# Moving the norm-factor sums and transposes of a hybrid attention layer later in TensorE's order, with one product and four operand rebuilds re-timed

## The chip, the cores and the metric

The kernel runs on one core of a Trainium2 chip. The metric is the device time of one execution in microseconds, as the median of several runs. Engines are named as in the profile: PE is TensorE (PEld its weight loads), DVE VectorE, ACT ScalarE, POOL GpSimd, and SP the engine that issues most DMAs. Each engine takes its instructions strictly in the order in which they were built.

## The reference

One encoder layer on x of 1024 tokens by 2048 features: RMSNorm, one input projection, eight retention heads, eight windowed attention heads, gates, an output projection, the residual and a last RMSNorm.

```python
h = rms_norm(x, norm_w)                 # x * rsqrt(mean(x*x) + eps) * w, per token
proj = h @ w_in                         # 2048 x 6656
rq, rk, rv, rg, aq, ak, av, ag = jnp.split(proj, splits, axis=-1)
y_ret = retention_branch(rq, rk, rv, ...) * silu(rg)
y_att = window_attention_branch(aq, ak, av, sink) * silu(ag)
out = rms_norm(x + concat([y_ret, y_att]) @ w_out, final_norm_w)
```

All of it is in float32; the kernel writes each factor of a big product as a rounded high part and a low rest and makes three matmuls of each pair.

## The kernel before, in words

**The projection.** `units` (L205) lists the work: a unit is one block of 512 output columns and one half (`part`) of the 2048 features. Columns and features of a unit are halved again, and a unit is made of seven products instead of eight, from sums of the quarters of the weight (`a11`, `a12`, `a21`, `a22`) and sums of the quarters of x (`comb[1]` to `comb[7]`, the tiles `c...` of the profile). "Operand" in this text means one such sum, split into high and low part: on the weight's side the tiles `wH` and `wL` (two of each, so operand n+2 waits until operand n has been used), on x's side `comb[i]`, which `put` (L1127) builds by a cast on ACT (L89) and a subtraction on DVE (L86). Each product takes 24 matmuls of 128x512 in four groups of six. Products 1, 6, 7 and 4 add up in the two PSUM banks X, products 2, 5 and 3 in the two banks Y; between two products on the same banks the sum so far has to be read out by DVE (`evict_rest`, L312, line L93 in the profile, tile `ct`), and PE may not write the bank until then.

**The start.** RMSNorm's factors are not known when the first matmul could run. So the first block, `akv`, is made by eight plain products (`plain`, L354): those on the first 512 tokens with unscaled x, then products 1 and 2 of the second block (`aq0`) and of the third (`aq1`) also unscaled (`early`, L390, banks `ax` and `pj`), then `plain` on the second 512 tokens with scaled x, then the other five products of the second and the third block (`rest`, L414). In `rest` the order is 5, 6, 3, 7, 4. Unscaled results wait in `ct` tiles until `scale_result` (L1131) multiplies them by the factors.

**The factors.** Half of the features come as columns and are squared on ACT (L498) and added on DVE (L93, tile `xx`); `sum_columns` (L507) has PE add them over the partitions by four matmuls with a vector of ones (L510). The other half comes as rows, eight tiles `xt`, squared with a running sum on ACT (L493). `factors_of` (L513) adds both on DVE (L516) and takes the power -0.5 on POOL (L517); `spread` (L1083) copies the factors over 128 columns (L1085); `turn_rows` (L1087) has PE transpose them (L1089, four small matmuls) and ACT copy the result into the tile `rows` (L1090), by which DVE then scales x (`scale`, L1092, line L1094). All this is done twice, first for the second half of the tokens, then for the first.

**The order.** `advance()` (L990) is called after every group of six matmuls of the projection, and each call is one step of a clock. The table of `at(n, ...)` calls (L1149 to L1214) says after which step each piece of work of the start is written into the program; where a call issues matmuls, that also is its place between PE's groups. Steps 1 to 16 are `plain` on the first half, 17 to 32 `early`, 33 to 48 `plain` on the second half, 49 to 68 `rest` of the second block, 69 to 88 that of the third. PE, SP and POOL keep the written order throughout; ACT and DVE keep it until step 66 (`BY_HAND`, L55), and after that the build orders them. `keep(0)` (L519) stores the finished x operands for later, 1 MB at a time; `second_part` (L539) loads the other half of x; `mixed` (L208) builds the weight operands of the second and the third block and, by `then`, reloads each weight quarter once it is free. `rotate` (L559) applies the rotary turn for the attention heads, in pieces that wait `idle(5)` steps between their loads and their first multiplication.

Of the kernel before, what the change touches and what calls it, by code (L numbers as in the profile page):

```python
# [59 lines left out]
def hybrid_layer_kernel(  # L60
# [34 lines left out]
    def sub(dst, a, b):  # L95
        return nc.vector.tensor_tensor(out=dst, in0=a, in1=b, op=ALU.subtract)
# [7 lines left out]
    def behind(it, ins):  # L104

        if it and clock[0] >= BY_HAND:
            tc.keep_in_program_order(ins)
# [4 lines left out]
    def half(i):  # L112
        return slice(i * HALF, (i + 1) * HALF)
# [9 lines left out]
    def start(job):  # L123
        if next(job, True) is None:
            jobs.append(job)
# [4 lines left out]
    def idle(n):  # L130
        for _ in range(n):
            yield
# [59 lines left out]
    def operand(src, pinned=False):  # L192
        wH, wL = (wp.tile([P, M, 2 * P], F32R, name=n, tag=n, bufs=AHEAD) for n in ("wH", "wL"))
        behind(pinned, nc.scalar.copy(out=wH, in_=src))  # L194
        low(wL, src, wH)
        return wH, wL
# [8 lines left out]
    units = [(part, b) for part, blocks in PHASES for b in blocks]  # L205
    w_next = {}

    def mixed(a, then):  # L208

        a11, a12, a21, a22 = (a[q] for q in QUARTERS)  # L210
        s2 = wp.tile([P, M, 2 * P], F32, name="s2", tag="s2")
        sub(a11, a11, a21)
        yield
        add(a21, a21, a22)
        yield
        op = [wp.tile([P, M, 2 * P], F32R, name=n, tag=n, bufs=AHEAD) for n in ("wH", "wL")]
        nc.scalar.copy(out=op[0], in_=a21)
        yield
        sub(s2, a22, a11)
        yield  # L220
        low(op[1], a21, op[0])
        then(2, 1)
        yield op
        yield operand(s2)
        sub(s2, a12, s2)
        then(1, 2)
        yield
        yield operand(s2)
        op = operand(a11)
        then(1, 1)  # L230
        yield op
        op = operand(a22)
        then(2, 2)
        yield op

    def then_of(u):

        def then(n, k):
            if u + 1 < len(units):
                w_next[n, k] = quarter(*units[u + 1], n, k)  # L240
            else:
                place_free(n, k)

        return then

    def operands():

        for u in range(2, len(units)):
            a, then = dict(w_next), then_of(u)
            if u == 2:  # L250
                yield from (op for op in mixed(a, then) if op)
                continue
            a11, a12, a21, a22 = (a[q] for q in QUARTERS)
            yield operand(a11)
            op = operand(a12)
            s2 = wp.tile([P, M, 2 * P], F32, name="s2", tag="s2")
            behind(True, sub(a11, a11, a21))
            sub(s2, a22, a11)
            yield op
            yield operand(s2, True)  # L260
            add(a21, a21, a22)
            op = operand(a21)
            then(2, 1)
# [12 lines left out]
            then(2, 2)  # L276
            yield op
# [68 lines left out]
    ops, ready = operands(), deque()  # L346
    unscaled, rows_of = [], []
    first_banks = {}
# [65 lines left out]
    def rest(b):  # L414

        if b not in held_of:
            first_scaled(b)
        held = held_of[b]
        Y, X = [pj(), pj()], [pj(), pj()]
        for i in (5, 6, 3, 7, 4):  # L420
            if b != units[1][1] or i == 4:
                prepare()
            bank = X if i in ON_X else Y
            products(i, bank, ready.popleft(), comb[i], i in (5, 6), True, lambda a: evict_rest(b, i, a, bank[a], held))
# [64 lines left out]
    def load_first(q, s, m, k0=0, n=M):  # L489
        q.dma_start(out=src0[:, s, k0:k0 + n, half(m)], in_=x_f[s, m][:, k0:k0 + n])  # L490
# [16 lines left out]
    def sum_columns(m, pt):  # L507

        for t in range(4):
            nc.tensor.matmul(pt[:, t:t + 1], columns[m][:, 0, blk(t)], ones, start=True, stop=True)  # L510
        nc.vector.tensor_copy(out=ssx[:, 0, 4 * m:4 * m + 4], in_=pt[:, 0:4])
# [47 lines left out]
    def rotate(pool, table, sets):  # L559

        for m in range(2):
            cs = [pool.tile([P, HALF], F32, name=f"rt{k}") for k in range(2)]
            for k in range(2):
                nc.sync.dma_start(out=cs[k], in_=table[:, k, half(m)])
            for of in sets:
                ts = [pool.tile([P, HALF], F32, name=f"rx{k}") for k in range(2)]
                for t, runs in zip(ts, of):
                    n = runs[0][2]
                    for i, (c, r, _) in enumerate(runs):
                        nc.sync.dma_start(out=t[i * n:(i + 1) * n], in_=pr[c][r:r + n, half(m)])  # L570
                yield from idle(5)
                n = of[0][0][2]
                u = slice(0, n * len(of[0]))
                for t, f in zip(ts, cs):
                    behind(True, nc.vector.tensor_tensor(out=t[u], in0=t[u], in1=f[u], op=ALU.mult))
                yield
                add(ts[0][u], ts[0][u], ts[1][u])
                yield from idle(2)
                for i, (c, r, _) in enumerate(of[0]):
                    nc.sync.dma_start(out=pr[c][r:r + n, half(m)], in_=ts[0][i * n:(i + 1) * n])  # L580
                yield
# [415 lines left out]
    u0, u1, u2 = units[:3]  # L997
    a11 = wp.tile([P, M, 2 * P], F32, name="a11", tag="a11")
# [63 lines left out]
    def load_quarter(n, k):  # L1062
        w_next[n, k] = quarter(*u1, n, k)
# [2 lines left out]
    load_quarter(1, 1)  # L1066
    load_first(nc.sync, 0, 1)
    load_first(nc.sync, 1, 1)
    for t in (4, 5, 6, 7):
        load_row(t)  # L1070
    load_quarter(1, 2)
    load_row(0)
    load_row(1)
    early_quarter(1)
# [12 lines left out]
    def turn_rows(m, pt):  # L1087
        for t in range(4):
            nc.tensor.transpose(pt[:, blk(t)], factors[m][:, blk(t)], ident)  # L1089
        nc.scalar.copy(out=both[:, half(m)], in_=pt)  # L1090
# [43 lines left out]
            nc.vector.tensor_tensor(out=e, in0=e, in1=rows_of[0], op=ALU.mult)  # L1134
            stores.append((True, to, e))

    mixed_first = mixed(w_next, then_of(1))

    def step(n=1):
        for _ in range(n):  # L1140
# [5 lines left out]
    def at(n, what, *args):  # L1146
        plan.setdefault(n, []).append((what, args))

    at(7, lambda: ready.append(operand(w_next[1, 1])))  # L1149
    for n, m in ((8, 0), (11, 1)):  # L1150
# [4 lines left out]
            if i < 3:  # L1155
                at(n + i, square_columns, m, i + 1)
        at(n + 3, add_columns, m, 4)
    at(13, lambda: sum_columns(0, first_banks[0, 1][0]))
    for n, t in ((13, 4), (14, 5), (15, 6), (15, 7), (18, 0), (19, 1), (21, 2), (22, 3)):
        at(n, square_row, t)  # L1160
    at(16, lambda: sum_columns(1, first_banks[0, 1][1]))
    at(16, factors_of, 4, 8)
    at(16, lambda: ready.append(operand(w_next[1, 2])))
    at(16, spread, 1)
    at(19, lambda: turn_rows(1, first_banks[0, 2][0]))
    at(19, hold_second)
    at(19, second_half, 0, "scale")
    at(20, lambda: ready.append(operand(early_w[1])))
    at(21, load_quarter, 2, 1)
    at(23, hold_third)  # L1170
    for k in range(2 * M):
        at(20 + k, second_half, k, "high")
        if k + 1 < 2 * M:
            at(20 + k, second_half, k + 1, "scale")
        at(20 + k, second_half, k, "low")
    at(23, factors_of, 0, 4)
    at(24, spread, 0)
    at(24, lambda: ready.append(operand(early_w[2])))
    at(25, load_quarter, 2, 2)
    at(26, lambda: turn_rows(0, first_banks[u1[1], 2][0]))  # L1180
    at(28, scale_result)
    at(31, scale_result)
    at(37, scale_result)
    at(48, scale_result)
    for k in range(M):
        at(33 + k // 2, scale, 0, k, 0)
    for n in (29, 30, 40, 40, 42, 47, 51):
        at(n, step)
    for j in range(2):
        at(35 + j, sum_of, 5, j)  # L1190
        at(38 + j, sum_of, 6, j)
        at(40 + j, put, 5, j)
        at(45 + j, put, 6, j)
        at(49 + j, sum_of, 7, j)
        at(51 + 2 * j, put, 7, j)
    for n, i in ((40, 5), (45, 6), (51, 7)):
        plan[n].insert(0, (hold, (i, 0)))
    at(44, first_scaled, u1[1])
    at(52, step)
# [7 lines left out]
    at(60, step)  # L1207
    at(61, put, 4, 1)
    for j in range(2):
        at(62 + j, put, 1, j)  # L1210
        at(66 + j, put, 2, j)
    at(62, lambda: start(keep(0)))
    at(69, lambda: start(second_part()))
    at(112, lambda: start(decays()))  # L1214

    def opening():
# [336 lines left out]
    for u in range(len(OUT)):  # L1553
# [4 lines left out]
        for group in LAST if u == 3 else [(i,) for i in PRODUCTS]:  # L1558
            i = group[0]
# [12 lines left out]
            for at, (p, t, j, q) in enumerate(order):  # L1572
# [7 lines left out]
                k = 2 * j + q  # L1580
# [92 lines left out]
```

## Time and profile before

| | |
|---|---|
| median of 3 runs | 1516.34 us (1514.03 to 1517.34) |
| the profiled execution | 1515.38 us, its span 1513.5 us |
| PE busy | 98% of the span |
| DVE, ACT, POOL busy | 74%, 45%, 10% |
| DMA | 316 MB moved, 209 GB/s on average |

A timeline row gives the start, the length, engine, line, operation and tiles, and in square brackets the idle time just before it with what ended that. The windows view gives busy microseconds of each engine in a stretch, with the number of instructions, then the granted PE clock as a share of full speed, the DMA engines' share and GB/s. The view of waits gives, for an engine and a line, whom it waited for, the sum, the number of times and the longest. The rows themselves stand in the prediction.

### The profile page before, as it was taken

The page shows a single profiled execution, that of the slowest core. Times are in us where ns is not written, and L with a number is a line of the kernel's source. Part 1 is how long each engine was busy: PE and PEld are TensorE (multiplying, and loading weights), DVE is VectorE, ACT ScalarE, POOL GpSimd, SP SyncE. Part 2 cuts the span into 40 slices and gives each one's busy share as a digit, 9 for nine tenths or more (in the row PEclk, how much of TensorE's full clock was granted, in tenths as well). Part 3 has the DMA queues.
Part 4 walks back from the last instruction along what each step waited for, and adds up shares of the span by engine and source line. Part 5 has one row for each costly group of instructions (what it writes and reads, how often), then busy time and mean ns, then how long its engine had stood idle before and what let it go on. Part 6 is the DMA issues. An engine that isn't in the chain of part 4 may idle for free.

```text
span 1513.5 us, 19947 instructions
## 1 busy us (share of the span) xinstructions
PE 1484.5 (98%) x7112; PEld 1247.4 (82%) x7112; DVE 1122.6 (74%) x1933; ACT 675.2 (45%) x1093; POOL 149.0 (10%) x176
## 2 busy tenths in 40 slices
PE   9999999999999999999999999999999999999997
PEld 7777888788888888888888788887888878888886
DVE  6897794557768576757988889887656956776766
ACT  7432363224545453533444444444444554542425
POOL 0000001111010000011211100001211102020001
PEclk9999999999999999999999999999999999999999
DMA  8249667888575526798767665689887799495656
GB/s 333 70 139 375 250 222 200 222 204 253 163 215 195 202 97 224 271 324 202 161 173 173 161 197 165 188 290 333 219 246 181 176 207 205 90 208 170 216 175 255
DMA packets 139779, 316.00 MB, mean 209 GB/s; under 512 B 31392, under 2 KB 52256, under 8 KB 130848
## 3 DMA queue, kind: packets, MB, share of 16 engines
q1 hardware_dynamic: 116064, 264.37, 52.5%
q0 software_dynamic: 19728, 36.71, 16.5%
q10 hardware_dynamic: 3888, 13.65, 2.7%
q8 instruction: 56, 0.92, 0.3%
q14 instruction: 43, 0.35, 0.1%
HBM read 195.92 MB, written 127.14 MB: 213 GB/s over the span
## 4 chain that ended last, share of the span: by engine, by line
PE 86%; DVE 5%; DMA 4%; issue 2%; ACT 1%; SPq 1%; POOL 1%; POOLq 0%; DVEq 0%; ACTq 0%
PE pj L102 22%; PE pj L100 22%; PE pj L101 22%; PE ax L101 5%; PE ax L102 5%; PE ax L100 5%; PE ax L882 2%; PE pj L369 1%; DMA pr<-ct 1%; PE ax L669 1%; DVE wL L86 1%; DMA yt<-mix 1%; PE ax L852 1%; DVE c L86 1%; PE ax L933 1%
## 5 line engine op out<-in xcount | busy, mean ns | idle before, releaser
L100 PE MATMUL pj<-c,wH 128*128 128x512 f32 x1384 | 549.1, 397 | 7.5 <-DVE ct L93 4.9
L102 PE MATMUL pj<-c,wL 128*128 128x512 f32 x1384 | 542.1, 392 | 4.9 <-DVE wL L86 4.8
L101 PE MATMUL pj<-c,wH 128*128 128x512 f32 x1384 | 540.6, 391 | 0.0
L102 PEld LDWEIGHTS pj<-c,wL 128*128 128x128 f32 x1384 | 260.6, 188 | 63.6 <-DVE wL L86 8.4
L100 PEld LDWEIGHTS pj<-c,wH 128*128 128x128 f32 x1384 | 260.9, 189 | 58.1 <-issue 5.1
L101 PEld LDWEIGHTS pj<-c,wH 128*128 128x128 f32 x1384 | 260.8, 188 | 49.4
L86 DVE TENSOR_TENSOR wL<-a,wH 128x1024 fp32r<-128x1024 f32 x151 | 184.1, 1220 | 102.3 <-ACT wH L194 52.4
L194 ACT CAST wH<-a 128x1024 fp32r<-128x1024 f32 x121 | 127.1, 1050 | 168.7 <-PE pj L101 134.2
L336 ACT COPY ct<-pj 128x512 f32<-128x512 f32 x184 | 106.9, 586 | 199.3 <-PE pj L102 194.1
L93 DVE TENSOR_TENSOR ct<-pj,ct 128x512 f32<-128x512 f32 x170 | 113.2, 686 | 49.4 <-PE pj L102 46.4
L309 POOL DMA_DIRECT2D pr<-ct x88 | 78.0, 957 | 527.1 <-DVE ct L93 429.8
L86 DVE TENSOR_TENSOR wL<-s,wH 128x1024 fp32r<-128x1024 f32 x56 | 68.4, 1221 | 57.8 <-ACT wH L194 49.9
L100 PE MATMUL pj<-wH,c 128*128 128x512 f32 x224 | 88.0, 393 | 1.4 <-ACT wH L89 1.4
L101 PE MATMUL pj<-wL,c 128*128 128x512 f32 x224 | 87.8, 392 | 0.8 <-DVE wL L86 0.8
L102 PE MATMUL pj<-wH,c 128*128 128x512 f32 x224 | 87.9, 392 | 0.0
L101 PE MATMUL ax<-wL,c 128*128 128x512 f32 x208 | 81.0, 390 | 0.0
L102 PE MATMUL ax<-wH,c 128*128 128x512 f32 x208 | 80.9, 389 | 0.0
L100 PE MATMUL ax<-wH,c 128*128 128x512 f32 x208 | 80.9, 389 | 0.0
L194 ACT CAST wH<-s 128x1024 fp32r<-128x1024 f32 x50 | 52.5, 1051 | 13.6 <-PE pj L101 8.6
L89 ACT CAST wH<-a 128x1024 fp32r<-128x1024 f32 x28 | 29.5, 1053 | 62.0 <-PE pj L102 35.0
L100 PEld LDWEIGHTS pj<-wH,c 128*128 128x128 f32 x224 | 42.5, 190 | 10.7 <-ACT wH L89 1.8
L659 ACT ACTIVATE s<-s,nm 128x385 f32<-128x385 f32 (+1 forms) x64 | 37.6, 589 | 30.2 <-DVE nm L654 27.3
(229 smaller groups left out, 2136.8 us busy)
## 6 DMA issues: line engine op xcount, KB each, us to landing
a<-in_w_in_dram SPq DMA_DIRECT2D x103, 512.0 KB, 5.7
kept<-c SPq DMA_DIRECT2D x28, 1024.0 KB, 7.0
c<-kept SPq DMA_DIRECT2D x28, 1024.0 KB, 8.3
pr<-ct SPq DMA_DIRECT2D x88, 256.0 KB, 5.1
pr<-ct POOLq DMA_DIRECT2D x88, 256.0 KB, 5.9
a<-in_w_out_dram SPq DMA_DIRECT2D x18, 512.0 KB, 4.4
rx<-pr SPq DMA_DIRECT2D x64, 128.0 KB, 5.2
ysrc<-pr ACTq DMA_DIRECT2D x16, 512.0 KB, 5.7
```

The lines of the kernel that those rows point to most:

```text
L86: return nc.vector.tensor_tensor(out=dst, in0=src, in1=high.bitcast(F32), op=ALU.subtract)
L89: behind(pinned, nc.scalar.copy(out=dst_h, in_=src))
L93: nc.vector.tensor_tensor(out=dst, in0=a, in1=b, op=ALU.add)
L100: nc.tensor.matmul(po, aH, bH, start=first, stop=False, **kw)
L101: nc.tensor.matmul(po, aH, bL, start=False, stop=False, **kw)
L102: nc.tensor.matmul(po, aL, bH, start=False, stop=last, **kw)
L194: behind(pinned, nc.scalar.copy(out=wH, in_=src))
L309: nc.gpsimd.dma_start(out=dst, in_=t, accum_op=ALU.add)
L336: nc.scalar.copy(out=t, in_=bank)
L369: nc.tensor.matmul(banks[a], w[:, q, blk(a)], c[:, q], start=first and j == 0, stop=last and j == 2)
L659: nc.scalar.activation(out=s[:, 0:w + 1], in_=s[:, 0:w + 1], func=AF.Exp, scale=-1.0, bias=nm, accum_out=den)
L882: nc.tensor.matmul(p, k_tok[:, c // 2, :, c % 2], vd[:, c, d], start=True, stop=True)
```

## The change

Seven things are edited, all but two of them in the table of steps:

- `sum_columns` goes from steps 13 and 16 to 15 and 18, the first `factors_of` and `spread` from 16 to 18, the first `turn_rows` from 19 to 21, the second from 26 to 30, the second `factors_of` and `spread` from 23 and 24 to 25 and 26; the multiplications of the second half by the factors go two steps later.
- The operand from weight quarter `a12` of the second block is built at step 13 instead of 16, and SP loads that quarter ahead of four of the rows of x instead of behind them.
- `scale_result` is called at 31, 37, 43 and 47 instead of 28, 31, 37 and 48.
- x operand 1 is rebuilt (`put`) at 39 and 40 instead of 62 and 63, x operand 2 at 69 and 70 instead of 66 and 67; the sums 6 and `put(5)` move by one step.
- In the third block `rest` takes the products in the order 5, 6, 7, 3, 4 instead of 5, 6, 3, 7, 4, and `mixed` builds that block's weight operands in the same order (`seventh_first`), with its reload of `a11` ahead of that of `a12`.
- `second_part` starts at 72 instead of 69.
- `rotate` waits six steps instead of five.

```diff
@@ rest
-        for i in (5, 6, 3, 7, 4):
+        for i in (5, 6, 3, 7, 4) if b == units[1][1] else (5, 6, 7, 3, 4):
@@ rotate
-                yield from idle(5)
+                yield from idle(6)
@@ loads
+    load_quarter(1, 2)
     for t in (4, 5, 6, 7):
         load_row(t)
-    load_quarter(1, 2)
@@ the table of steps
-    at(13, lambda: sum_columns(0, first_banks[0, 1][0]))
+    at(13, lambda: ready.append(operand(w_next[1, 2])))
+    at(15, lambda: sum_columns(0, first_banks[0, 1][0]))
...
-    at(26, lambda: turn_rows(0, first_banks[u1[1], 2][0]))
+    at(30, lambda: turn_rows(0, first_banks[u1[1], 2][0]))
...
+        at(39 + j, put, 1, j)
...
-        at(62 + j, put, 1, j)
-        at(66 + j, put, 2, j)
+        at(69 + j, put, 2, j)
...
-    at(69, lambda: start(second_part()))
+    at(72, lambda: start(second_part()))
```

What it does to the built order is shown at three places. The first is PE at the end of `plain` on the first half of the tokens, where the sums over the partitions stand (L369 is a matmul of `plain`, L510 the sums, `ax` the first product of the second block). Before:

```order
L369 MATMUL pj<-c_215,w 128x512 x6
L510 MATMUL pj<-ones,xx 128x1 x4
L369 MATMUL pj<-c_215,w 128x512 x18
L510 MATMUL pj<-ones,xx 128x1 x4
L100 MATMUL ax<-c_214,wH 128x512
```

After it (line numbers past L207 are higher by 7 there; L376 is the matmul of `plain`, L517 the sums):

```order
L376 MATMUL pj<-c_215,w 128x512 x18
L517 MATMUL pj<-ones,xx 128x1 x4
L376 MATMUL pj<-c_215,w 128x512 x6
L100 MATMUL ax<-c_214,wH 128x512
L101 MATMUL ax<-c_214,wH 128x512
```

The first group of sums has gone behind twelve more matmuls of `plain`; the second, which stood ahead of the first `ax` matmul, stands twelve matmuls into that product. The second place is PE in the third block's two early products, where the second transpose of the factors stands (L1089, after it L1096). It leaves the middle of product 1 (`ax` matmuls on `c_214`):

```order
 L101 MATMUL ax<-c_214,wH 128x512
 L102 MATMUL ax<-c_214,wL 128x512
-L1089 MATMUL pj<-ident,factors 128x128 x4
 L100 MATMUL ax<-c_214,wH 128x512
 L101 MATMUL ax<-c_214,wH 128x512
```

and goes into the middle of product 2 (`pj` matmuls on `c_215`):

```order
 L101 MATMUL pj<-c_215,wH 128x512
 L102 MATMUL pj<-c_215,wL 128x512
+L1096 MATMUL pj<-ident,factors 128x128 x4
 L100 MATMUL pj<-c_215,wH 128x512
 L101 MATMUL pj<-c_215,wH 128x512
```

That is 24 matmuls later. The third place is DVE while PE makes products 3, 7 and 4 of the second block (L93 on `pj` reads out the banks; the first pair is product 3's, the second product 7's; `c_214` is x operand 1, `c_215` operand 2, `c_883` operand 4). Before:

```order
L86 TENSOR_TENSOR wL<-a_262,wH 128x1024
L96 TENSOR_TENSOR tt<-src,tt 128x1024 x2
L86 TENSOR_TENSOR c_215<-src,c_215 128x1024
L86 TENSOR_TENSOR c_883<-tt,c_883 128x1024
L93 TENSOR_TENSOR ct<-pj,ct 128x512 x2
L86 TENSOR_TENSOR wL<-a_549,wH 128x1024
L86 TENSOR_TENSOR c_883<-tt,c_883 128x1024
L86 TENSOR_TENSOR c_214<-src,c_214 128x1024 x2
L93 TENSOR_TENSOR ct<-pj,ct 128x512 x2
```

After it (operand 4 is `c_887` there, L419 is `first_scaled` of the third block):

```order
L86 TENSOR_TENSOR wL<-a_262,wH 128x1024
L96 TENSOR_TENSOR tt<-src,tt 128x1024 x2
L419 TENSOR_TENSOR ct<-ax,rows 128x512
L86 TENSOR_TENSOR c_887<-tt,c_887 128x1024
L93 TENSOR_TENSOR ct<-pj,ct 128x512 x2
L86 TENSOR_TENSOR wL<-a_539,wH 128x1024
L86 TENSOR_TENSOR c_887<-tt,c_887 128x1024
L93 TENSOR_TENSOR ct<-pj,ct 128x512 x2
```

Operand 1 has left the place ahead of product 7's read-out (it now stands behind the sums for product 6, before `c_704`, operand 5), operand 2 has gone behind it, and half of `first_scaled` has come in. Further on, the longer wait in `rotate` puts everything that attention and retention issue on PE two groups (twelve matmuls) later against the projection, from the first transposes of attention to the end of retention; ACT and DVE come out in another order there, and in the same one after retention but for a few places.

More of the change, by code (lines that the diff above doesn't have):

```diff
@@ L206, in hybrid_layer_kernel, with mixed @@
     w_next = {}
-    def mixed(a, then):
+    def mixed(a, then, seventh_first):
         a11, a12, a21, a22 = (a[q] for q in QUARTERS)
@@ L224, in mixed, with seventh @@
         yield operand(s2)
+        def seventh():
+            op = operand(a11)
+            then(1, 1)
+            return op
+        if seventh_first:
+            yield seventh()
         sub(s2, a12, s2)
@@ L228, in mixed @@
         yield operand(s2)
-        op = operand(a11)
-        then(1, 1)
-        yield op
+        if not seventh_first:
+            yield seventh()
         op = operand(a22)
@@ L250, in operands @@
             if u == 2:
-                yield from (op for op in mixed(a, then) if op)
+                yield from (op for op in mixed(a, then, True) if op)
                 continue
@@ L1135, in scale_result @@
             stores.append((True, to, e))
[L1137 removed]
+    mixed_first = mixed(w_next, then_of(1), False)
     def step(n=1):
@@ L1157, in hybrid_layer_kernel @@
         at(n + 3, add_columns, m, 4)
-    at(13, lambda: sum_columns(0, first_banks[0, 1][0]))
+    at(13, lambda: ready.append(operand(w_next[1, 2])))
+    at(15, lambda: sum_columns(0, first_banks[0, 1][0]))
     for n, t in ((13, 4), (14, 5), (15, 6), (15, 7), (18, 0), (19, 1), (21, 2), (22, 3)):
         at(n, square_row, t)
[L1161 to L1167, printed above, removed]
+    at(18, lambda: sum_columns(1, first_banks[0, 1][1]))
+    at(18, factors_of, 4, 8)
+    at(18, spread, 1)
+    at(21, lambda: turn_rows(1, first_banks[0, 2][0]))
+    at(20, hold_second)
     at(20, lambda: ready.append(operand(early_w[1])))
+    at(21, second_half, 0, "scale")
     at(21, load_quarter, 2, 1)
@@ L1171, in hybrid_layer_kernel @@
     for k in range(2 * M):
-        at(20 + k, second_half, k, "high")
+        at(22 + k, second_half, k, "high")
         if k + 1 < 2 * M:
[L1174 to L1177, printed above, removed]
+            at(22 + k, second_half, k + 1, "scale")
+        at(22 + k, second_half, k, "low")
     at(24, lambda: ready.append(operand(early_w[2])))
     at(25, load_quarter, 2, 2)
-    at(26, lambda: turn_rows(0, first_banks[u1[1], 2][0]))
[L1181 to L1184, printed above, removed]
+    at(25, factors_of, 0, 4)
+    at(26, spread, 0)
+    at(30, lambda: turn_rows(0, first_banks[u1[1], 2][0]))
+    for n in (31, 37, 43, 47):
+        at(n, scale_result)
     for k in range(M):
         at(33 + k // 2, scale, 0, k, 0)
-    for n in (29, 30, 40, 40, 42, 47, 51):
+    for n in (29, 30, 39, 40, 43, 47, 51):
         at(n, step)
@@ L1190, in hybrid_layer_kernel @@
         at(35 + j, sum_of, 5, j)
-        at(38 + j, sum_of, 6, j)
-        at(40 + j, put, 5, j)
+        at(37 + j, sum_of, 6, j)
+        at(39 + j, put, 1, j)
+        at(41 + j, put, 5, j)
         at(45 + j, put, 6, j)
@@ L1195, in hybrid_layer_kernel @@
         at(51 + 2 * j, put, 7, j)
-    for n, i in ((40, 5), (45, 6), (51, 7)):
+    for n, i in ((41, 5), (45, 6), (51, 7)):
         plan[n].insert(0, (hold, (i, 0)))
```

## The prediction

> **What bounds the kernel now.** I read the head of the page first, then the view of PE's waits, then the windows, and last the timelines of PE, DVE and ACT around each wait.
>
> ```profile
> span 1513.5 us, 19947 instructions
> PE 1484.5 (98%) x7112; PEld 1247.4 (82%) x7112; DVE 1122.6 (74%) x1933; ACT 675.2 (45%) x1093; POOL 149.0 (10%) x176
> PE pj L100 <- DVE ct L93: 4.9, 3, 3.2
> PE pj L102 <- DVE wL L86: 4.8, 5, 1.5
> PE pj L100 <- ACT wH L194: 2.6, 1, 2.6
> PE pj L1089 <- DVE factors L1085: 2.5, 2, 1.9
> PE pj L510 <- DVE xx L93: 0.8, 1, 0.8
> ```
>
> PE is the bound: 1513.5 - 1484.5 = 29 us of the span is all that it stands still. The change removes no matmul, so only those stops can give time, and the half-speed stretches behind them. The windows tell where the start's stops lie.
>
> ```profile
> 0.00:60.00 60.00, 55.40 (x254) 45.35 (x255) 43.68 (x63) 41.22 (x60) 2.75 (x8) 0.97 0.66 246
> 60.00:112.00 52.00, 48.77 (x209) 39.88 (x208) 48.91 (x54) 20.02 (x22) 0.00 (x0) 0.97 0.34 111
> ```
>
> The columns are the stretch, its length, busy PE, PEld, DVE, ACT and POOL, the granted clock, the DMA share and GB/s. From 60 to 112 DVE is busy 48.9 of 52 us: there it is DVE that PE follows. The granted clock of 0.97 in both shows that part of each ran slowly. The stops themselves, on PE:
>
> ```profile
> 25.58 1.02 PE L510 MATMUL pj<-ones,xx 128*128 128x1 f32 x8 [0.78 <-DVE xx L93]
> 36.38 0.63 PE L1089 MATMUL pj<-ident,factors 128*128 128x128 f32 x4 [0.53 <-DVE factors L1085]
> 48.50 1.02 PE L1089 MATMUL pj<-ident,factors 128*128 128x128 f32 x4 [1.93 <-DVE factors L1085]
> 49.74 0.63 PE L101 MATMUL ax<-c,wH 128*128 128x512 f32 x1
> 51.45 0.63 PE L102 MATMUL ax<-c,wL 128*128 128x512 f32 x1
> 58.94 10.89 PE pj L369 x48
> 102.07 0.39 PE L102 MATMUL pj<-c,wL 128*128 128x512 f32 x1
> 105.69 0.47 PE L100 MATMUL pj<-c,wH 128*128 128x512 f32 x1 [3.23 <-DVE ct L93]
> 135.85 0.47 PE L100 MATMUL pj<-c,wH 128*128 128x512 f32 x1 [1.08 <-DVE ct L93]
> ```
>
> At full pace a matmul takes 10.89 / 48 = 0.227 us. Between 49.74 and 51.45 there are four of them in 1.71 us, 0.43 each: after the stop of 1.93 us PE ran at half pace. The granted clock of 0.97 over 60 us and over 52 us is 1.8 and 1.6 us lost, one such time in each stretch; I take 1.7 each. The last two rows are product 4 waiting for the read-out of product 7, on the same banks, in the second block (105.69) and in the third (135.85).
>
> **The sums and transposes, part by part.** Each is put behind matmuls that don't need it, so the stop goes if its input is ready by then.
>
> ```profile
> 28.49 1.95 DVE L93 TENSOR_TENSOR xx<-xx 128x1024 f32<-128x1024 f32 x2
> 37.67 0.75 DVE L1094 SCALAR_TENSOR_TENSOR src<-src,vec_t,rows 128x512 f32<-128x512 f32 x1 [1.43 <-ACT rows L1090]
> 39.29 1.23 DVE L86 TENSOR_TENSOR wL<-b,wH 128x1024 fp32r<-128x1024 f32 x1 [0.87 <-ACT wH L194]
> 40.43 0.74 DVE L1094 SCALAR_TENSOR_TENSOR src<-src,vec_t,rows 128x512 f32<-128x512 f32 x1
> 41.10 0.68 DVE L86 TENSOR_TENSOR b<-src,b 128x512 fp32r<-128x512 f32 x1
> 41.70 0.74 DVE L1094 SCALAR_TENSOR_TENSOR src<-src,vec_t,rows 128x512 f32<-128x512 f32 x1
> ```
>
> ```profile
> 28.05 1.04 ACT L493 ACTIVATE junk<-xt 128x1024 bf16<-128x1024 f32 x1
> 29.22 1.06 ACT L493 ACTIVATE junk<-xt 128x1024 bf16<-128x1024 f32 x1
> 33.58 1.06 ACT L194 CAST wH<-a 128x1024 fp32r<-128x1024 f32 x1
> 34.53 1.06 ACT L493 ACTIVATE junk<-xt 128x1024 bf16<-128x1024 f32 x1
> 37.05 0.59 ACT L1090 COPY rows<-pj 128x512 f32<-128x512 f32 x1 [0.18 <-PE pj L1089]
> 45.79 1.02 POOL L517 TENSOR_TENSOR rms<-rms,neg_half 128x4 f32<-128x4 f32 x1 [11.75 <-DVE rms L516]
> ```
>
> What an instruction costs its engine is the distance to the next start, since ends overlap: 1.14 for a `wL` (39.29 to 40.43), 0.67 for a scaling, 0.6 for a low part, 0.95 for a cast on ACT (33.58 to 34.53), 1.17 for a square.
>
> First sums: the input is there at about 25.6 and twelve matmuls (2.7 us) now cover it, so the stop of 0.8 to 0.9 us goes. PE gets to the second sums at 32.3. Their input slips: the early operand of `a12` costs ACT a cast ahead of the squares and stands in DVE's queue ahead of the last two `xx` additions, so these end near 32.1 instead of 30.4. That fits by 0.2 us.
>
> First transpose: the squares of rows 4 to 7 begin at 29.0 instead of 28.05 and end near 33.8; with rms, the power on POOL (1.02) and the copy the factors are there at 35.7. PE comes at 37.3: the stop of 0.5 to 0.7 goes. What it costs is that `rows`, at 37.05 before, now waits on ACT behind three squares and a cast and comes at 39.2, so DVE's first scaling starts at 39.8 instead of 37.67, 2.1 later.
>
> Second transpose: from 37.3 PE has the transposes (0.4), 18 + 24 + 12 = 54 matmuls (12.3), and is there at 50.0. DVE has from 39.8 five scalings and four low parts of x one read-out pair (1.2) and one `wL` ahead of the sum on L516, which falls at 48.2; POOL ends at 49.4 and the factors are there at 50.0. Wait 0 to 0.3 us in place of 1.93, and without its half-speed stretch. This is the tightest place of the change. Together PE begins `plain` on the second tokens at 53.5 instead of 58.78, 5.2 us sooner: 0.9 + 0.7 + 1.9 + 1.7.
>
> **What is late next.** PE's lead meets DVE's queue. From the first scaling to the read-out of product 7, DVE runs nearly without a break:
>
> ```profile
> 58.37 1.37 DVE L93 TENSOR_TENSOR ct<-pj,ct 128x512 f32<-128x512 f32 x2 [0.68 <-PE pj L102]
> 72.37 2.36 DVE L86 TENSOR_TENSOR c<-tt,c 128x1024 fp32r<-128x1024 f32 x2 [3.09 <-ACT c L89]
> 102.58 2.37 DVE L86 TENSOR_TENSOR c<-src,c 128x1024 fp32r<-128x1024 f32 x2
> 104.85 1.29 DVE L93 TENSOR_TENSOR ct<-pj,ct 128x512 f32<-128x512 f32 x2
> ```
>
> Before, this takes 104.85 - 37.67 = 67.2 us, with 0.87 + 0.68 + 3.09 = 4.6 of it idle (the 0.87 ahead of the first `wL<-b`, which now comes before the scaling). The other two gaps wait for PE, directly or through ACT, whose cast stands behind a copy of `plain`'s result; with PE 5.2 us sooner both close. The work itself: that `wL` leaves the stretch (-1.1), one of the two low parts of operand 2 leaves it (-1.1), one multiplication of `first_scaled` enters (+0.6). Operand 1's 2.27 us at 102.58 only moves forward into what was the gap of 3.09. So the read-out begins at 39.8 + 67.2 - 4.6 - 1.7 = 100.7, and product 4 at 101.4 instead of 105.69: **4.3 us** of the 5.2. PE would be there at 98.3 (53.5 + 21.8 of `plain` + 4 x 5.45 + about 1 of short waits for `wL`), so it still stops for some 3 us, and since a stop of 1.93 brought the half pace, I keep that loss of 1.7 behind it.
>
> The Trainium skill, page "TensorE: Matmul & The Clock Gate", section "Why this matters for your kernels", asks for no PE gaps over about 3 us, one idle window putting the clock back to half. By it a stop of 1.93 us costs nothing more, PE's lead would be 3.5 instead of 5.2, and DVE's queue would still set the 4.3. The trace differs: 1.93 us was enough here.
>
> Third block: product 4 there no longer follows 7, so its 1.08 (pitch 1.47 against 0.23, 1.2 lost) goes. In its place 7 follows 6 on the banks X. What that costs is not in the trace; the nearest rows are a read-out with DVE free and the next product's first matmul.
>
> ```profile
> 117.81 1.37 DVE L93 TENSOR_TENSOR ct<-pj,ct 128x512 f32<-128x512 f32 x2 [1.08 <-PE pj L102]
> 118.29 0.39 PE L100 MATMUL pj<-c,wH 128*128 128x512 f32 x1
> ```
>
> The first bank is read out at about 118.5, so a product on it would start 0.3 late; at the other end is the 1.2 of now. I take 0.3, since DVE is idle up to 2.6 us between read-outs there. That is 0.9 more: **5.2 in all**.
>
> **Edits that I cost at nothing.** Scaling the results later: the read-outs need those `ct` tiles only after their stores, and even the third call ends on DVE near 73, two us before PE has the next results to copy (75.3), with the banks not needed until 80.8. `second_part` three steps later and operand 2 behind it: SP waits at the reload of x until operand 2 is split, and the reload of `a11` is queued behind; but `a11` is now asked for one product (5.4 us) sooner and needed only at 136, and the reload of x not before the first phase ends. If that cover failed, this wait of ACT, a few us ahead of PE's use now, would become a PE stop of 1 to 2 us.
>
> ```profile
> 136.02 1.05 ACT L194 CAST wH<-a 128x1024 fp32r<-128x1024 f32 x1 [5.82 <-DMA a<-in_w_in_dram]
> ```
>
> `rotate`: in the built order DVE's first rotary row has the same neighbours as before, so I take no change there. What remains is attention and retention two groups later, with ACT and DVE reordered. The one large stop among them:
>
> ```profile
> 843.81 1.65 ACT L959 ACTIVATE y<-y,mv,rstd 128x128 f32<-128x128 f32 x4 [0.75 <-DVE mv L957]
> 846.44 0.50 PE L100 MATMUL pj<-c,wH 128*128 128x512 f32 x1 [2.62 <-ACT wH L194]
> 847.89 0.79 PE L102 MATMUL pj<-c,wL 128*128 128x512 f32 x1 [0.72 <-DVE wL L86]
> ```
>
> The last row's length of 0.79 shows half pace again. The weight's cast stands behind two sets of normalizations on ACT. In the new order it stands between them (1.65 sooner), but the normalizations come two groups, 2.7 us, later against the projection. I take no change, between -5.4 (2.8 + 0.9 in starts, and 1.7 of half pace) and +5.4 (one more such stop).
>
> **The sum.** Profiled execution 1515.38 - 5.2 = 1510.2; it lies 0.96 under the median of the runs shown, so the median should be 1516.34 - 5.2 = **1511.1**.
>
> **The rivals.** (a) The stop at 843 goes, or the remaining stop before product 4 keeps full pace: 1.7 to 5.4 better, 1505.7 to 1509.4. For it: the cast's new place, and the stop's new length. Against: the 1.93 us that cooled PE, and the 2.7 us delay. Chance 0.17. (The Trainium skill's page above, same section, has its limit at about 3 us, just where this stop would be.) (b) The second transpose still waits: its slack is under 0.3 us, and every microsecond on ACT or DVE from 28 to 48 counts. A wait of 2 with half pace gives back up to 3.7 at PE and delays the gap at 72: 1512 to 1515, I say 1514. Chance 0.14. (c) The change does nothing at the end, because PE's lead is all taken by DVE's queue or a `ct` tile not yet stored: 1516. Chance 0.07. (d) Slower: the two groups' delay puts normalizations ahead of weight casts at two more of the eight heads. Each costs 5.4 as at 843, and it decides from the first one on, which undoes the gain (1516.5, chance 0.13); two make 1516.34 - 5.2 + 10.8 = 1521.9, chance 0.07. For it: ACT and DVE are reordered over 700 us. Against: the view of waits counts one such wait in all eight heads.
>
> **How the numbers follow.** The forecast has the rest, 0.42. A measurement here can tell about 0.2%, 3 us, so faster means under 1513.3. Faster: 0.40 of the forecast, 0.17 of (a), 0.07 of (b): 0.64. Slower, over 1519.4: 0.08, from (d). The same: 0.28. The range from 1506.0 to 1517.0 leaves out the two heads of (d) and the best third of (a), 0.13.
>
> **What would show it.** Right: no stop at the first sums and first transpose, under 0.5 us at the second, full clock near 50, `plain` on the second tokens at about 53.5; product 4 of the second block near 101.4 after a stop of about 3 us; third block without its 1.08. Wrong: a wait on L1096 over 1 us, a read-out of product 7 after 104, a new wait of PE between 110 and 200, or waits for `wH` behind normalizations at several heads.

## The result, and the profile after

| | before | after |
|---|---|---|
| median of the runs | 1515.2 us (4 runs) | 1527.76 us (4 runs, 1524.46 to 1529.63) |
| profiled execution | 1515.38 us, span 1513.5 | 1524.46 us, span 1522.3 |

The ratio is 1.0079, with a 95% interval of 1.0057 to 1.0101: the change makes the kernel 12 us slower, where I had forecast 1511.1. Times of one kernel spread over up to 11 us, and with them the mean clock that each run lists, so the ratios below carry the comparisons, and single profiles only show where time lies.

The head of the page after, and rows of the view of PE's waits (reason: total us, times, longest):

```profile
span 1522.3 us, 19931 instructions
PE 1486.2 (98%) x7112; PEld 1247.1 (82%) x7112; DVE 1122.3 (74%) x1933; ACT 673.4 (44%) x1093; POOL 149.7 (10%) x176
PE pj L100 <- ACT wH L194: 12.3, 5, 9.0
PE pj L102 <- DVE wL L86: 6.3, 8, 2.1
PE pj L100 <- DVE ct L93: 3.2, 3, 2.9
PE ax L100 <- ACT qbH L89: 1.7, 1, 1.7
PE pj L1096 <- DVE factors L1092: 0.2, 1, 0.2
```

PE stands still for 36.1 us instead of 29.0. The waits for the factors (2.5, now 0.2) and for `xx` (0.8) are gone, as forecast; in their place a row that was 2.6 us, waiting for ACT's cast of a weight, has 12.3, and 9.0 of it is one stop. Four windows after, and in the second block the window of before that answers to the fourth, tell where:

```profile
0.00:60.00 60.00, 58.46 (x273) 49.33 (x274) 43.07 (x62) 41.82 (x61) 3.73 (x8) 1.00 0.63 237
60.00:112.00 52.00, 48.05 (x203) 38.74 (x202) 51.73 (x59) 20.34 (x22) 0.00 (x0) 0.97 0.40 125
150.00:260.00 110.00, 108.49 (x477) 88.89 (x476) 76.01 (x100) 47.69 (x64) 7.28 (x8) 1.00 0.70 228
700.00:1070.00 370.00, 354.79 (x1846) 301.97 (x1845) 307.95 (x672) 161.33 (x281) 38.76 (x39) 0.98 0.73 202
```

```profile
700.00:1070.00 370.00, 363.38 (x1915) 311.36 (x1915) 315.10 (x690) 166.50 (x287) 40.57 (x41) 1.00 0.75 209
```

The first 60 us came out better (58.46 us busy against 55.40, and a full clock). From 700 to 1070 PE is idle 15.2 us instead of 6.6, at a clock of 0.98 instead of 1.00: that is retention, whose order I had passed over with "no change". PE, DVE, ACT and GpSimd after, at the long stop:

```profile
1053.95 0.79 PE L100 MATMUL pj<-c,wH 128*128 128x512 f32 x1 [9.02 <-ACT wH L194]
1041.82 0.71 DVE L158 STREAM_TRANSPOSE ct<-y 128x512 f32<-128x512 f32 x1
1043.24 0.70 DVE L158 STREAM_TRANSPOSE ct<-y 128x512 f32<-128x512 f32 x1
1041.13 0.59 ACT L343 COPY ct<-pj 128x512 f32<-128x512 f32 x1 [5.82 <-issue]
1052.37 0.59 ACT L343 COPY ct<-pj 128x512 f32<-128x512 f32 x1 [10.64 <-DMA pr<-ct]
1052.85 1.05 ACT L194 CAST wH<-s 128x1024 fp32r<-128x1024 f32 x1
1045.75 0.92 POOL L316 DMA_DIRECT2D pr<-ct  x1 [14.24 <-DVE ct L93]
```

PE waits for the weight `wH<-s`; its cast stands behind a copy in ACT's queue; the copy (of a finished bank to a `ct` tile) waits 10.64 us until a store `pr<-ct` has landed, so until its `ct` tile is free. Ten us earlier DVE has taken two of the eight tiles within 1.4 us for the two normalized halves of one head (L158). The store that the copy waits for is GpSimd's, issued at 1045.75: a row of the chain that ended last (start, length, what) names it, and so does the view of its line, L316, under who waited for it (us, times).

```profile
1045.75 6.54 DMA pr<-ct
  ACT ct L343: 10.6, 1
```

In the built program the copy at 1052.37 is given the very tile that the copy at 1041.13, the first bank's, had filled; the other seven are given to two read-outs, two copies, a rotated key and the two normalized halves. So the second bank has to wait until the first one's tile is read out again (1044.66), stored (1045.75) and landed (1052.29). The first copy was late for the same reason: it starts 0.07 us after the store `kz<-ct` of its tile had landed, which SP had issued 14.2 us before. SP's rows of the stretch after that issue (the first is a gather of four transfers):

```profile
1027.50 7.45 SPq L164 DMA_DIRECT2D v_tok<-vz  x4
1035.05 1.46 SPq L814 DMA_DIRECT2D kz<-ct  x1
1036.82 4.22 SPq L314 DMA_DIRECT2D pr<-ct  x2
1045.35 3.09 SPq L972 DMA_DIRECT2D mix<-ct  x1
1050.01 0.52 SPq L972 DMA_DIRECT2D mix<-ct  x1
```

The five stores of `ct` tiles among them stand behind that gather, but none of them is the one that the copy waits for. In e1 below the first store to `mix` is issued 13.8 us after its transpose, without such a stop. The records show the clock at one half for three windows of 3.41 us, 10.24 us in all, from 1047.69 to 1057.93. Most of that lies in the stop itself; PE worked at half pace for 4.0 us behind it, which costs about 2 us.

A single profile can also be read by leads: how much sooner the same matmul, counted in PE's order, starts than in the profile of before. From the matmul that before starts at 1040 to the one at 1070, after goes from 2.0 us behind to 11.9 us behind: the stop and the half pace together cost 9.9 us more than before's own stop of 1.7 us near 1045.

### The profile page after: what moved, and what is told of

Its sections match the earlier page's. It is cut to its first block, busy times and chain, and to the rows that moved or that the text cites. A ratio compares the mean times of both kernels' runs of the same rounds, so it can differ in the third digit from the quotient of the medians.

```text
span 1522.3 us, 19931 instructions
## 1 busy us (share of the span) xinstructions
PE 1486.2 (98%) x7112; PEld 1247.1 (82%) x7112; DVE 1122.3 (74%) x1933; ACT 673.4 (44%) x1093; POOL 149.7 (10%) x176
## 4 chain that ended last, share of the span: by engine, by line
PE 81%; DVE 9%; issue 3%; DMA 3%; ACT 2%; POOL 1%; SPq 1%; ACTq 0%; POOLq 0%; DVEq 0%
PE pj L102 20%; PE pj L100 20%; PE pj L101 20%; PE ax L101 5%; PE ax L102 5%; PE ax L100 5%; DVE wL L86 2%; PE ax L889 1%; PE ax L676 1%; DMA q<-pr 1%; DMA pr<-ct 1%; PE ax L859 1%; DVE c L86 1%; DVE ct L93 1%; PE pj L376 1%
## 5 line engine op out<-in xcount | busy, mean ns | idle before, releaser
L100 PE MATMUL pj<-c,wH 128*128 128x512 f32 x1384 | 550.7, 398 | 15.5 <-ACT wH L194 12.3
L93 DVE TENSOR_TENSOR ct<-pj,ct 128x512 f32<-128x512 f32 x170 | 113.1, 686 | 67.2 <-PE pj L102 56.6
L316 POOL DMA_DIRECT2D pr<-ct x88 | 78.0, 964 | 516.9 <-DVE ct L93 421.1
L101 PEld LDWEIGHTS pj<-wL,c 128*128 128x128 f32 x224 | 42.1, 188 | 9.8 <-DVE wL L86 1.1
```

The costliest lines, as they stand in the source:

```text
L93: nc.vector.tensor_tensor(out=dst, in0=a, in1=b, op=ALU.add)
L100: nc.tensor.matmul(po, aH, bH, start=first, stop=False, **kw)
L101: nc.tensor.matmul(po, aH, bL, start=False, stop=False, **kw)
L316: nc.gpsimd.dma_start(out=dst, in_=t, accum_op=ALU.add)
```

## The experiments

Theory 1: the sixth step in `rotate`, which brings attention and retention two groups later, costs everything, and the start gains what I forecast. Theory 2: the start's lead itself makes later stores and tiles late. Theory 3: only both together cost. The ratios to the kernel before (measured beside each) are below; e2, e4 and e11 have 4 to 6 runs, the others 11 or 12.

| run | what | median us | ratio, 95% interval |
|---|---|---|---|
| e1 | after, five steps in `rotate` | 1514.08 | 0.9988 (0.9976 to 1.0000) |
| e2 | before, six steps | 1529.52 | 1.0094 (1.0078 to 1.0110) |
| e3 | after, retention two steps sooner | 1516.73 | 1.0010 (0.9998 to 1.0021) |
| e4 | e1, retention two steps later | 1525.21 | 1.0062 (1.0046 to 1.0077) |
| e5 | e1, operand 1 late as before | 1512.77 | 0.9985 (0.9973 to 0.9997) |
| e6 | e1, third block in the order of before | 1515.29 | 0.9993 (0.9980 to 1.0006) |
| e7 | after, own tiles for the normalized results | 1517.92 | 1.0011 (0.9999 to 1.0023) |
| e8 | e1, operand 1's low parts on GpSimd | 1515.95 | 0.9997 (0.9981 to 1.0013) |
| e9 | e5, operand 2 and `second_part` as before too | 1513.53 | 0.9990 (0.9977 to 1.0004) |
| e10 | e9, retention two steps sooner | 1511.89 | 0.9982 (0.9969 to 0.9996) |
| e11 | after, seven steps | 1523.06 | 1.0049 (1.0036 to 1.0062) |
| e12 | e1, own tiles as in e7 | 1514.24 | 0.9988 (0.9975 to 1.0000) |

**The sixth step by itself (e1, e2).** This is e1's edit of the changed kernel; e2 has the reverse in the kernel before.

```diff
-                yield from idle(6)
+                yield from idle(5)
```

> The changed kernel with the wait in rotate back at five steps: every engine's order from the third block on is that of the kernel before. Theory 1 (the sixth step, which brings attention and retention two groups later, costs all): the start's gain of 5.2 us is left, so 1510 us (1507 to 1513) beside 1515.2 before, PE idle some 24 us, no stop of over 4 us and full clock near 1045. Theory 2 (the start's lead of 5 us itself makes stores and ct tiles late afterwards): the stop near 1045 or others of its kind stay, 1522 to 1528. Theory 3 (only the two together cost): 1510 as well; the next run parts it from theory 1.

> The kernel before with the wait in rotate at six steps and nothing else. Theory 1: all the loss without the gain: 1527.8 + 5.2 = 1533 us (1529 to 1536), with a stop of about 9 us of PE near 1050 and half clock behind it. Theory 2: as the kernel before, 1514 to 1517. Theory 3 (the sixth step is harmless where PE has no lead): 1514 to 1518 as well, and then the run before this one is at 1510.

Measured: without the step the rest of the change makes the kernel 1.8 us faster by the ratio (0 to 3.6); the step alone makes the kernel before 14.2 us slower. Together that is 12.4, and the change measures 12.0: the parts add within their uncertainty, so theories 2 and 3 fall. The step alone shows the same stop of PE (8.5 us) near 1057. But theory 1 is only half right: of the 5.2 us at the start 1.8 are there.

**Which of the two it is that comes late (e3, e4).**

```diff
                 nc.gpsimd.dma_start(out=rot, in_=rot_r)
                 while to_load:
                     yield
-                yield from idle(8)
+                yield from idle(6)
```

e3 has this in the changed kernel; e4 has `idle(10)` in e1.

> The changed kernel, with retention begun two steps sooner, so that attention alone stands two groups later. By the windows of PE's busy time the changed kernel is idle 8.6 us more than before between 700 and 1070 and has two more windows of half clock there (3.4 us), against 2.9 us more idle between 150 and 700. Theory 1 with the loss in retention: 1527.8 - 12 = 1516 us (1513 to 1518), no long stop near 1045, the short stops near 153 and 437 still there. Theory 1 with the loss in attention, or theory 2: 1524 us or more.

> The wait in rotate back at five steps, and retention alone begun two steps later. Loss in retention: 1510 + 12 = 1522 us (1519 to 1525), with the long stop near 1045. Loss in attention: 1508 to 1513. Theory 2 says nothing else than for the first of these runs, 1522 to 1528.

Measured against e1: retention late alone costs 11.2 us (1.0062 - 0.9988), attention late alone 3.3. e4's view of PE's waits has the long row again, 11.6 us with one of 8.2 for `wH`; e3's has none over 2.6, and a wait of 2.1 us for `qbH`, like after's 1.7. The loss is retention's for the most part. Attention's share lies near 440: from the matmul that before starts at 430 to the one at 450 the lead falls by 3.0 us in after and by 3.3 in e3, around the wait for `qbH`. Why `qbH` is late there was not followed.

**The `ct` tiles (e7, and e12 as its control).** The transposed results of the normalizations get two tiles of their own. To make room, the rotation table of retention leaves out its second half, and its first serves both halves of the tokens, so the values of retention are not the reference's; the number and the shapes of the instructions stay, and the load of the table is half as large. The two main places of the edit, with others cut (...):

```diff
-            rot = ret.tile([P, 2, S], F32, name="rot")
+            rot = ret.tile([P, 2, HALF], F32, name="rot")
...
-                z = ct()
+                z = ret.tile([P, HALF], F32, name="z", tag="z", bufs=2)
                 turn_half(z, y.rearrange("p c e -> p (c e)"))
...
```

> The changed kernel (rotate at six steps), with two tiles of their own for the transposed results of the normalizations, which otherwise take two of the eight ct tiles. To make room, retention's rotation table holds its first half alone, used for both halves of the tokens (so the values of retention differ). Theory 1a (the long stop near 1045 is a ct tile that isn't free: two normalizations' results wait for their stores while the projection's copies want tiles): the stop of 9.4 us falls under 3 us, with one window of half clock instead of three: 1527.8 - 6.5 - 3.4 = 1518 us (1515 to 1521). Theory 1b (the stores are late in SP's queue whatever the tiles, so ACT waits all the same): the stop stays over 6 us and the time is 1523 to 1528.

> The control for the own tiles: rotate at five steps, with the same two tiles of their own for the normalizations' results and the same halved rotation table (so the values of retention differ). If the own tiles take away only what the sixth step had brought, there is nothing to take away here: 1514 us (1512.5 to 1515.5). If they gain the same 10 us here, they say nothing about the sixth step: 1504 us or so.

Measured: with six steps the own tiles take off 10.3 us (1.0079 - 1.0011), with five steps nothing. ACT of e7 at the place of the long stop:

```profile
1036.79 1.27 ACT L343 COPY ct<-pj 128x512 f32<-128x512 f32 x2 [1.69 <-PE pj L102]
1043.00 1.05 ACT L194 CAST wH<-s 128x1024 fp32r<-128x1024 f32 x1 [4.95 <-DVE s L96]
1044.58 1.05 ACT L194 CAST wH<-a 128x1024 fp32r<-128x1024 f32 x1 [0.53 <-PE pj L101]
```

Both copies follow PE at once, one pair at 1036.79 instead of one copy at 1041.13 and one at 1052.37, and the cast is not held up: 1043.00 instead of 1052.85. PE's largest gap from one start to the next here is 2.2 us instead of 9.4, and between the matmuls of 1040 and 1070 e7 loses 0.7 us of its lead instead of 9.9. In e7's built program the two copies are given two tiles whose stores had been issued 12 us before. SP's gather of `v_tok` takes its 6.65 us in e7 as well, so it is the tiles, not the queue alone, that made ACT wait. Ten `ct` tiles for all users, instead of two set apart, were not tried. In e1 the two transposes stand 15 us apart, and the two copies between them are given two different tiles:

```profile
1021.12 0.71 DVE L158 STREAM_TRANSPOSE ct<-y 128x512 f32<-128x512 f32 x1
1036.47 0.70 DVE L158 STREAM_TRANSPOSE ct<-y 128x512 f32<-128x512 f32 x1
```

**Later or sooner (e10, e11).**

> The run before this one, with retention begun two steps sooner. If a later start of retention costs because the work has less time before its due point, a sooner one costs nothing or gains 1 to 3 us: 1509 to 1512. If what counts is only how its groups fall against the projection's blocks, two steps either way lose alike: 1518 us or more, with a new stop of over 4 us somewhere between 800 and 1070.

> The changed kernel with one more step still, seven in rotate, so that attention and retention stand four groups later than before. If delay itself costs, 1530 us or more. If what counts is how the groups fall against the projection, it may come out anywhere from 1512 to 1540, and the stop of 9.4 us near 1045 changes place or length.

Neither theory fits both. Two steps sooner, on the kernel of e9 (`idle(6)` as in e3's diff), measures 0.9982 against e9's 0.9990: no loss, and alone not told apart from e9. Seven steps cost less than six, 1.0049 against 1.0079, but the ring of tiles runs dry in e11 too, now ahead of DVE's transpose itself:

```profile
1047.54 0.71 DVE L158 STREAM_TRANSPOSE ct<-y 128x512 f32<-128x512 f32 x1 [6.87 <-DMA pr<-ct]
```

PE's starts there lie 10.6 us apart. So delay isn't priced by the step. What costs, by e7 and e12 and in keeping with e11's row, is two results of one head wanting tiles while the projection wants them too. Why the longer stop of e11 comes with a smaller loss stays open.

**What of the start's gain is missing (e5, e6, e9).** In e1 PE's stops in the first 160 us, beside those that went, are:

```profile
88.25 0.50 PE L102 MATMUL pj<-c,wL 128*128 128x512 f32 x1 [0.67 <-DVE wL L86]
94.38 0.50 PE L102 MATMUL pj<-c,wL 128*128 128x512 f32 x1 [0.39 <-DVE wL L86]
102.54 0.47 PE L100 MATMUL pj<-c,wH 128*128 128x512 f32 x1 [2.88 <-DVE ct L93]
109.84 0.50 PE L102 MATMUL pj<-c,wL 128*128 128x512 f32 x1 [1.15 <-DVE wL L86]
```

To these come 1.9 us near 153 (the lead there falls from 4.1 to 2.2). Ahead of the 109.84 DVE has operand 2's low part at 107.43 and only then the weight's at 108.56. Near 153 ACT's queue has turned round against before; e1's rows, and then those of before:

```profile
153.08 0.59 ACT L343 COPY ct<-pj 128x512 f32<-128x512 f32 x1 [8.54 <-PE pj L102]
153.56 1.05 ACT L194 CAST wH<-a 128x1024 fp32r<-128x1024 f32 x1
```

```profile
154.65 1.06 ACT L194 CAST wH<-a 128x1024 fp32r<-128x1024 f32 x1 [6.09 <-DVE a L93]
157.22 0.59 ACT L336 COPY ct<-pj 128x512 f32<-128x512 f32 x1 [1.51 <-PE pj L102]
```

e1's cast has had its input since 151.65 (DVE's addition at 150.43, 1.22 long), and waits 1.9 us behind a copy that waits for PE. Three runs undo parts (each on top of e1; the diffs are cut to the lines that count):

```diff
e5:
-        at(39 + j, put, 1, j)
+        at(62 + j, put, 1, j)
e6:
-        for i in (5, 6, 3, 7, 4) if b == units[1][1] else (5, 6, 7, 3, 4):
+        for i in (5, 6, 3, 7, 4):
e9 (with e5's line):
-        at(69 + j, put, 2, j)
+        at(66 + j, put, 2, j)
-    at(72, lambda: start(second_part()))
+    at(69, lambda: start(second_part()))
```

e6 also has `mixed` yield the seventh's operand in the order of before.

> The changed kernel with rotate at five steps, and operand 1 rebuilt where the kernel before has it: its two low parts (1.14 us each on DVE) stand ahead of the read-out of product 7 again, and ACT's cast of the weights near 153 stands ahead of the copies again, as before. If DVE's queue sets product 4 of the second block, it starts at 104.8 instead of 102.5; the stop of 1.8 us near 153 goes: together 1514.1 + 2.3 - 1.8 = 1514.6 us (1513.5 to 1516). If the place of operand 1 doesn't matter for product 4 (some other wait sets it), 102.5 stays and the time is 1512.3 us (1511 to 1513).

> Rotate at five steps, and the third block's products in the order of before (7 ahead of 4). The prediction's step: product 4 waits some 1.2 us for the read-out of 7 again, and the 0.36 lost between 6 and 7 comes back: 0.9 more, 1515 us (1514 to 1516). Rival: the time is made up at the stop near 153, where PE waits for a weight cast that doesn't depend on PE's lead: 1514 us, and that stop is 0.9 shorter.

> Of the change only the later sums and transposes (with the scaled results behind them) and the third block's order stay: rotate at five steps, operands 1 and 2 and second_part where the kernel before has them. Theory (the edits costed at nothing bring stops of their own: operand 1's place turns ACT's copy and cast round near 153, 1.8 us of stops, operand 2's low part stands ahead of a weight's near 108, 1.3 us): both stops go, product 4 of the second block still starts near 102.6, and the time is 1514.1 - 2.5 = 1511.6 us (1510 to 1513). Rival (those stops are covered by slack that the read-outs have): 1513 to 1515.

Product 4 of the second block starts at 102.74 in e5 and 102.55 in e9, as in e1: operand 1's place makes no difference, as e5's second theory had it, and the first fell. DVE's rows of e1, with operand 1's parts early, and of e5, with them late, tell why:

```profile
50.59 0.43 DVE L1092 COPY factors<-rms 128x512 f32<-128x512 f32 x1 [0.91 <-POOL rms L524]
67.42 1.22 DVE L86 TENSOR_TENSOR c<-src,c 128x1024 fp32r<-128x1024 f32 x1
69.69 1.22 DVE L86 TENSOR_TENSOR c<-src,c 128x1024 fp32r<-128x1024 f32 x1
101.71 1.28 DVE L93 TENSOR_TENSOR ct<-pj,ct 128x512 f32<-128x512 f32 x2
```

```profile
99.65 2.34 DVE L86 TENSOR_TENSOR c<-src,c 128x1024 fp32r<-128x1024 f32 x2
101.92 1.27 DVE L93 TENSOR_TENSOR ct<-pj,ct 128x512 f32<-128x512 f32 x2
```

From the factors to the read-out DVE has no gap in either; it does the same work in another order. Of the stop near 153 e5 has 1.1 us left and e9 nothing. The stop near 109 is gone in both, but not by the edits: e5 still has operand 2's low part (107.12) ahead of the weight's (108.26). PE comes later there, since behind product 4's stop the clock is at one half until 105.97 in e5 and 107.70 in e9. It is so in all the profiles: those with full clock behind product 4 (e1, e3, e4, e8) have a stop of 0.9 to 1.2 us there (109 to 111), and those with half clock there (after, e5, e6, e7, e9 to e12) have none. DVE, busy up to there but for 0.43 us, sets that point too.

Yet e9's ratio is no better than e1's. By its trace it is 1.1 us ahead of e1 at the matmul that before starts at 250, which the ratios can't tell. One thing takes back part of what the missing stops give: the waits for `wL` near 88 and 94 have gone as well, so PE comes to product 4 sooner and its one stop is 5.07 us instead of 2.88, with half clock for 6.83 us (from 100.87 on; 5.15 of it behind the stop), where e1's has none. Over the twelve runs of each the median clock is 0.9935 in e9 and 0.996 in e1, which is 3.8 us of 1510. That the longer stop is the cause of the lower clock in all twelve is argued, not shown.

e6 measures 0.8 us over e1 by the ratios, within the uncertainty, and its trace says that this is not the third block's order: with the order of before, product 4 waits 0.20 us there (131.19), not 1.08, and e6 gains 0.9 us of lead in that block as e1 does. In before DVE has two multiplications of `second_part` ahead of the read-out of product 7:

```profile
131.37 2.48 DVE L549 SCALAR_TENSOR_TENSOR src<-src,vec_t,rows 128x1024 f32<-128x1024 f32 x2
135.02 1.28 DVE L93 TENSOR_TENSOR ct<-pj,ct 128x512 f32<-128x512 f32 x2
```

In e6, where `second_part` starts three steps later, that read-out (130.36) follows PE, with DVE idle for 2.68 us before it. e9 has `second_part` as before and the new order, and gains 0.8. So either edit seems to be enough by itself; no run changes `second_part` alone.

**A try at DVE's queue (e8).** The lines that matter, in `put` (the other operands go on as in e1):

```diff
+        if i == 1:
+            nc.scalar.copy(out=h, in_=of)
+            nc.gpsimd.tensor_tensor(out=l, in0=of, in1=h.bitcast(F32), op=ALU.subtract)
```

> Rotate at five steps, and operand 1's two low parts subtracted on GpSimd, idle there, instead of VectorE; all else in the same order. If DVE's queue sets product 4 of the second block, it starts up to 2.3 us sooner (100.3 instead of 102.5), its stop falls from 3 us to under 1, and no half clock follows: 1514.1 - 2.3 = 1511.8 us (1510 to 1513). Rival: GpSimd's subtractions are slow or slow VectorE down beside them, or come too late for the product that reads them: 1514 to 1518, with PE waiting for GpSimd.

The rival won: no gain, product 4 at 103.56. GpSimd's two subtractions, and two of DVE's that ran beside them:

```profile
61.62 17.31 POOL L1139 TENSOR_TENSOR c<-src,c 128x1024 fp32r<-128x1024 f32 x2 [11.04 <-ACT c L1138]
74.40 5.61 DVE L86 TENSOR_TENSOR c<-tt,c 128x1024 fp32r<-128x1024 f32 x2
```

What takes DVE 2.27 us takes GpSimd 17.3, and a pair of DVE's own beside it took 5.61 instead of 2.35.

## Why the prediction was wrong, point by point

**The sums and transposes: right.** No wait at the first sums (27.99) nor at the second (32.99), none at the first transposes (38.07), and 0.18 at the second. PE and DVE after:

```profile
32.99 1.02 PE L517 MATMUL pj<-ones,xx 128*128 128x1 f32 x8
38.07 0.60 PE L1096 MATMUL pj<-ident,factors 128*128 128x128 f32 x4
51.11 0.66 PE L1096 MATMUL pj<-ident,factors 128*128 128x128 f32 x4 [0.18 <-DVE factors L1092]
54.35 5.60 PE L376 MATMUL pj<-b,w 128*128 128x512 f32 x24
40.00 1.41 DVE L1101 SCALAR_TENSOR_TENSOR src<-src,vec_t,rows 128x512 f32<-128x512 f32 x2 [0.30 <-ACT rows L1097]
```

The first scaling is at 40.00 (39.8 forecast), the factors at 50.6 (50.0), `plain` on the second tokens at 54.35 (53.5, against 58.78 before). PE was 0.7 behind my times from the second sums on (32.3 forecast), so most of the 0.85 at the end was there before the transposes.

**DVE's queue: right in kind, mis-sized by 1.2 us.** Product 4 of the second block began at 102.58, where I said 101.4: a gain of 3.1 instead of 4.3. (0.2 of it is the later scaling.) I had closed DVE's gaps of 4.6 us and opened none, but the later second factors make one, the 0.91 us for which DVE waits for GpSimd's power (the row at 50.59 in e1; 50.62 after). The stop of some 3 us came as forecast (2.88). The third block's term held in size: 0.20 of waiting at product 7, 0.36 lost, 0.3 forecast. But I gave its 0.9 us to the new order alone, and e6 has them with the old one.

**"Edits that I cost at nothing": wrong for operand 1, operand 2 and `second_part`.** Those move no work off an engine, but they change who stands ahead of whom on DVE and ACT: 1.9 us are lost near 153, where e5 ties a part to operand 1 and e9 the whole to the three edits together. By e1's trace the lead is 3.1 us at product 4, 3.3 at the matmul that before starts at 114, 4.1 behind the third block and 2.2 behind 153; the ratio says 1.8 (0 to 3.6), against 5.2. The price of 1 to 2 us that I had written beside them for a failed cover was about right by luck: the cover that I named (the load of `a11`) was not the one that failed.

**"`rotate`: no change", and "I take no change, between -5.4 and +5.4": the step that decided.** The first row of the rotary work did keep its neighbours, but the step that costs is two groups' delay of retention, 11.2 us by e4, with attention's 3.3 by e3. I had bounded it by the one large stop in the trace of before, at 843, and that stop changed little. The bound was no bound: the stop at 1045 (9.0 us of waiting for a `ct` tile) has no row in the trace of before, since there the two transposes lie 15 us apart. **Rival (d)** had the side, and its 1521.9 for two heads was the nearest figure, but its mechanism, normalizations ahead of weight casts, is not what happened: it is a copy ahead of a cast, and a tile that isn't free. I had met that very resource, `ct` tiles not yet stored, only as a rival for the start (c).

**Rival (a) and the clock.** Whether the stop of 2.88 us before product 4 keeps full pace is not settled by its length. The same wait of 2.88 us is there in after and in e1: after, the records show half clock behind it for 3.41 us; in e1, none. The row of 102.54 in e1 lasts 0.47, that of 102.58 after 0.77. But keeping full pace gains nothing that lasts: at the matmul that before starts at 114, after and e1 are both 3.3 us ahead, since e1 then stops for 1.15 us near 109. So the 1.7 us that I kept in the sum was right for some runs, and the gain that (a) saw in full pace there was in none. The limit of about 3 us in the Trainium skill, "TensorE: Matmul & The Clock Gate", section "Why this matters for your kernels", is not borne out as a threshold here: 1.93 us brought half clock in before, and 2.88 did and did not.

## What to carry to other kernels

Where a change shifts a whole stage by a step, list the buffers that the stage shares with its neighbours, and look at when each user takes and frees one: the price of this shift was the ring running dry once, not the number of steps, and no row of the old trace showed it. An engine whose queue is in program order passes such a wait on to whatever stands behind the waiting instruction, here from a store to a copy to a weight's cast to TensorE. And when an engine is busy without a gap up to the point that counts, moving its work forward or back leaves that point where it is, and a stop that goes ahead of it comes back in the stop at that point.

## What the runs showed of the hardware

But for the last one, at the end of the program, half clock comes in whole windows of 3.41 us here (one, two or three of them: 3.41, 6.83, 10.24), and within one execution they begin at whole multiples of 3.413 us from one another (before: 17, 234, 348 and 428 windows after the first). The Trainium skill, "TensorE: Matmul & The Clock Gate", section "What's actually happening", has such a window, of 3413 ns and free-running, and the trace agrees. How a stop falls on that grid would explain why one of 2.88 us is followed by half clock in one execution and not in the next; that is argued, not shown. With the clock goes the spread of a kernel's time: e1's twelve runs go from 1509.03 us at a mean clock of 0.998 to 1516.54 at 0.994.

A subtraction of 128x1024 on GpSimd took 8.7 us beside a busy VectorE, against VectorE's 1.14 (e8).
